# The last 1024 down columns of an MLP go pair by pair in three of four cycles, and two vector operations are merged

## The chip, the cores and the metric

The kernel runs on one core of a Trainium2 chip as one program. Engines: TensorE (PE in the profile, its weight loads PEld), VectorE (DVE), ScalarE (ACT), GpSimd (POOL), and SyncE (SP), whose queue issues nearly all DMA transfers. PE reads its operands from SBUF and writes its sums to PSUM, which has eight banks of 128 x 512 fp32 numbers. The metric is the device time of one execution in microseconds (us); less is better.

## The reference, cut to what matters

A two-layer encoder trunk on x of 256 positions by 2048 channels, all fp32. Each layer has a mixer (not touched here) and then this MLP, with D_FF = 8192:

```python
def sq_relu_mlp(h, w_up, w_down):
    a = jnp.einsum('bsd,df->bsf', h, w_up)
    a = jnp.square(jax.nn.relu(a))
    return jnp.einsum('bsf,fd->bsd', a, w_down)
...
        x = x + sq_relu_mlp(rmsnorm(x, mlp_norm[i]), w_up[i], w_down[i])
    return rmsnorm(x, final_norm)
```

## The kernel before

**Precision.** Products are made in three matmuls each (mm3, L105): every operand is split into a rounded high part and the rest (hi, lo), and hi x hi, hi x lo, lo x hi are summed in one bank. ACT makes the high part (L73, L184), DVE subtracts it (L74, L185). So each weight loaded costs ACT one cast and DVE one subtraction.

**The MLP** (L631) runs twice, once a layer. Hidden columns are made in tiles of 128 ("up tile": accT, L655 to L685, one bank, 16 matmuls of 512 and 16 of 256 columns) and two such tiles make a pair q of 256 hidden rows (hidden, L695: scale, square, split, and the block sums xh, xl of a seven-product scheme). 32 pairs are taken in G = 4 cycles of C = 8. The down product of a pair is a 2 x 2 by 2 x 2 block product: two halves of hidden rows k, two halves of positions t (128 each), two column tiles n of 512. For the first 1024 of the 2048 output columns it is made by seven block products instead of eight (Q1, P2, Q3, Q5, Q7, Q6, Q4; L801 to L818), 21 matmuls, from the weight blocks (bh, bl, made in s_load, L722) and their sums (th, tl, made in s_sums, L733: four DVE additions in place in sraw, then two splits). They stay in seven banks for the whole cycle: four of the pool accp, three of the pool tpp, whose fourth bank is left to the up tiles. A step of the loop L793 is: up tile, three products of the pair before, second up tile, four products. After a cycle s_end (L751) copies Q1 with ACT and adds the seven banks to x with 12 DVE operations.

**The last 1024 columns** come after that (L821): for each of two column tiles n, `linear` (L110) goes over the cycle's 16 k-tiles with two sums of 512 columns (one for each t), 96 matmuls, then add_x (L224) adds the two banks to x. So 192 matmuls a cycle. A weight load is 1 MB (four k-tiles) and is split in two pieces of 1024 columns. In the last cycle one of its eight pairs goes by `rest` (L766), and in the last MLP the last column tile is done in halves with the final norm behind it (Final, L587). The final norm's gain gf is loaded by the POOL queue into a pool of its own before the last MLP (L1152 to L1154).

**What sets the order.** The program is laid out once, when it is built: a planner goes by the order of the text, but puts an instruction ahead on its engine's queue when its inputs and its buffer are there and earlier ones still wait. At run time each engine takes its queue in that fixed order and waits on semaphores. What can go ahead is set by buffers: three raw weight tiles, four hi and four lo pieces (L50 to L52), four staging tiles (tag stg), one each of sraw, bh, bl, th, tl, xh and xl, and eight banks.

Of the kernel before, what the change touches and what calls it, by code (L numbers as in the profile page):

```python
# [19 lines left out]
P = 128  # L20
# [8 lines left out]
PIECE = 2048  # L29
HALF = 1024  # L30


# [4 lines left out]
WHOLE = (1, 2)  # L37

SMALL = ["conv_w", "conv_b", "ln_g", "ln_b", "g_o", "conv_c", "q_g", "kv_g", "g_m0", "g_m1"]
SMALL_N = [8 * CONVK, 8, 8, 8, 16, 8 * 3, 4, 2, 16, 16]  # L40
# [3 lines left out]
def trunk_kernel(ctx, tc, x_in, x_t, small, w_in_e0, w_in_e, w_out_e, w_in_o, w_lat2, w_uqn, w_uqr, w_ukv, w_out_o,  # L44
                 w_up0, w_up1, w_ds0, w_ds1, w_dn0, w_dn1, g_fin, dft_s, dft_c, rope, out):
    nc = tc.nc
# [186 lines left out]
    class NormIn:  # L233


        def __init__(self, name, g):
            self.name, self.g = name, g
            self.act = act_tiles(16, name)
            self.ss = new_ss(name)
            self.r = None  # L240
# [346 lines left out]
    class Final:  # L587


        def __init__(self, gf):  # L590
            self.gf = gf
            self.ss = const.tile([P, 2, 5], F32, name="nfs")
            nc.vector.memset(self.ss[:, 0, 4:], 0.0)

        def part(self, t, i, a, b, gain=True):
# [34 lines left out]

    def mlp(ni, pend, w_up, w_ds, w_dn, nxt):  # L631

# [62 lines left out]
        def hidden(q, z):  # L695
# [13 lines left out]
            nc.vector.tensor_tensor(out=x[:, 3, :], in0=h[:, 3, :], in1=x[:, 2, :], op=ALU.subtract)  # L709
            xh = mp_.tile([P, 4, P], F32R, tag="xh", name="xh")  # L710
            xl = mp_.tile([P, 4, P], F32R, tag="xl", name="xl")
            split_from(x, xh, xl)
# [8 lines left out]

        def s_load(q):  # L722

            raw = mp_.tile([P, PIECE], F32, tag="sraw", name="sraw")
            nc.sync.dma_start(out=raw, in_=w_ds[q])
            bh = mp_.tile([P, 3, 512], F32R, tag="bh", name="bh")
            bl = mp_.tile([P, 3, 512], F32R, tag="bl", name="bl")
            r4 = raw.rearrange("p (a b) -> p a b", a=4)
            for a, b in ((0, 1), (1, 3)):
                split_from(r4[:, a + 1:b + 1, :], bh[:, a:b, :], bl[:, a:b, :])  # L730
            return r4, bh, bl

        def s_sums(r4):  # L733
            for o, i0, i1 in ((1, 1, 0), (0, 0, 2), (2, 1, 2), (3, 2, 3)):
                nc.vector.tensor_tensor(out=r4[:, o, :], in0=r4[:, i0, :], in1=r4[:, i1, :], op=ALU.add)  # L735
            th = mp_.tile([P, 4, 512], F32R, tag="th", name="th")
            tl = mp_.tile([P, 4, 512], F32R, tag="tl", name="tl")
            for a in (0, 2):
                split_from(r4[:, a:a + 2, :], th[:, a:a + 2, :], tl[:, a:a + 2, :])
            return th, tl  # L740
# [7 lines left out]
        def add(out, a, b, op=ALU.add):  # L748
            nc.vector.tensor_tensor(out=out, in0=a, in1=b, op=op)

        def s_end(b):  # L751


            v = stg.tile([P, 512], F32, tag="stg", name="cv", bufs=4)
            nc.scalar.copy(out=v, in_=b["Q1"])
            for q, t, n in (("Q1", 1, 0), ("P2", 1, 0), ("Q3", 1, 1), ("Q5", 1, 1), ("Q5", 0, 1)):
                add(xc(t, n), b[q], xc(t, n))
            u = stg.tile([P, 512], F32, tag="stg", name="cu", bufs=4)
            add(v, b["Q6"], v, ALU.subtract)
            add(u, b["Q7"], v, ALU.subtract)  # L760
            add(xc(0, 0), b["Q4"], xc(0, 0))
            add(xc(1, 1), xc(1, 1), v)
            add(xc(0, 0), xc(0, 0), u)
            add(xc(0, 1), xc(0, 1), u, ALU.subtract)

# [23 lines left out]
        for g in range(G):  # L789
# [29 lines left out]
            s_end(b)  # L819
            hT = [tuple(pair(g * C + k // 2)[:, i, (k % 2) * S:(k % 2 + 1) * S] for i in range(2)) for k in range(2 * C)]  # L820
            for n in (2, 3):  # L821
                if last and n == 3 and isinstance(nxt, Final):
                    linear(hT, list(range(16)), w_dn[2 * g + n - 2], 0, 512, halves=True, done=nxt.last, early=8)
                    st.close()
                    return {}
                acc = linear(hT, list(range(16)), w_dn[2 * g + n - 2], 0, 512, hooks=pend)
                add_x(acc, n)
                if last and n == 2:
                    rest(hT)
                    for m in (0, 1, 2):  # L830
                        nxt.stats(m)
                        pend[4 * m + 3] = [lambda m=m: nxt.chunk(m)]
                elif last:
                    nxt.stats(3)
                    pend = {3: [lambda: nxt.chunk(3)]}
# [31 lines left out]
    nxt = Lazy("n2", smv("g_o"))  # L867
    pend = mlp(ni, pend, w_up0, w_ds0, w_dn0, nxt)
    ni = nxt
# [281 lines left out]

    fp = ctx.enter_context(tc.tile_pool(name="fin", bufs=1))  # L1152
    gf = fp.tile([P, D], F32, name="gf")
    nc.gpsimd.dma_start(out=gf, in_=g_fin.broadcast_to([P, D]))  # L1154

    mlp(ni, pend, w_up1, w_ds1, w_dn1, Final(gf))


# [85 lines left out]
```

## Time and profile before

| | |
|---|---|
| median of 3 runs | 1956.17 us (1955.97 to 1957.41) |
| the profiled execution | 1957.39 us, span 1955.6 us |
| PE busy | 1943.4 us (99%), 9894 matmuls |
| PEld busy | 1651.3 us (84%) |
| DVE busy | 1569.8 us (80%), 2191 instructions |
| ACT busy | 1129.3 us (58%), 1579 instructions |
| POOL busy | 10.8 us (1%) |
| granted clock | 0.999 of full |
| HBM read | 370.27 MB, 190 GB/s over the span |

The span is what the profiler recorded on the core; the execution's own time has 1.8 us around it. Busy times are shares of the span of each engine by itself; engines work side by side. A matmul row shows when it was issued and a modelled length of 0.39 us that overlaps the next, so what one costs is read from the distance between starts. In a timeline, `x4` is a merged run of four, the bracket says how long the engine was idle ahead and what ended that.

### The profile page before, as it was taken

The numbers are of one execution on the slowest core, as the hardware profiler recorded it, in microseconds if no ns is written. First come the engines' busy times: TensorE is split into PE (matmuls) and PEld (weight loads), VectorE is DVE, ScalarE is ACT, GpSimd is POOL, SyncE is SP. The second block draws the span as 40 slices with busy tenths as digits, with TensorE's granted clock in tenths as the row PEclk, the third lists the DMA queues.
The fourth block names the chain that finished last, engine by engine and source line by source line (L and its number), as shares of the span: only waits on it lengthen the run. The fifth ranks groups of instructions, "written<-read, shape, count | busy, mean of one in ns | idle before, by whom it ended". The sixth has DMA issues, their size and how long they took to land.

```text
span 1955.6 us, 25251 instructions
## 1 busy us (share of the span) xinstructions
PE 1943.4 (99%) x9894; PEld 1651.3 (84%) x9894; DVE 1569.8 (80%) x2191; ACT 1129.3 (58%) x1579; POOL 10.8 (1%) x19
## 2 busy tenths in 40 slices
PE   9999999999999999999999999999999999999998
PEld 8887788888888888888888888888888888888887
DVE  7999778978896897887576666588968878896885
ACT  6787656645654664565554545466546645654653
POOL 0000000000000000000000000000000000000000
PEclk9999999999999999999999999999999999999999
DMA  8654555555556555454554546555565555555543
GB/s 294 213 173 162 207 191 194 194 196 183 201 188 211 197 197 199 174 198 167 164 183 146 189 169 242 191 173 196 191 215 194 195 200 187 194 192 207 185 169 129
DMA packets 55207, 374.00 MB, mean 191 GB/s; under 512 B 6064, under 2 KB 6448, under 8 KB 11824
## 3 DMA queue, kind: packets, MB, share of 16 engines
q1 hardware_dynamic: 54656, 370.69, 54.0%
q8 instruction: 77, 1.26, 0.3%
q0 software_dynamic: 144, 1.05, 0.1%
q10 hardware_dynamic: 288, 0.66, 0.1%
q14 instruction: 42, 0.34, 0.1%
HBM read 370.27 MB, written 2.10 MB: 190 GB/s over the span
## 4 chain that ended last, share of the span: by engine, by line
PE 97%; DMA 1%; DVE 1%; issue 0%; ACT 0%; SPq 0%; POOL 0%; POOLq 0%; DVEq 0%; ACTq 0%
PE accT L672 24%; PE acc L107 14%; PE acc L108 14%; PE acc L106 14%; PE accT L664 13%; PE Q L106 4%; PE Q L108 4%; PE Q L107 4%; PE tp L106 1%; PE tp L107 1%; PE tp L108 1%; PE P L107 1%; PE P L106 1%; PE P L108 1%; DMA raw<-in_w_in_e 1%; PE tp L197 1%
## 5 line engine op out<-in xcount | busy, mean ns | idle before, releaser
L74 DVE TENSOR_TENSOR wlo<-raw,whi 128x1024 fp32r<-128x1024 f32 (+1 forms) x572 | 687.9, 1210 | 300.3 <-ACT whi L73 299.8
L73 ACT CAST whi<-raw 128x1024 fp32r<-128x1024 f32 (+1 forms) x572 | 596.5, 1044 | 456.6 <-PE acc L108 291.3
L672 PE MATMUL accT<-n,whi 128*128 128x512 f32 x2048 | 512.5, 392 | 0.0
L672 PEld LDWEIGHTS accT<-n,whi 128*128 128x128 f32 x2048 | 376.1, 188 | 75.1
L664 PEld LDWEIGHTS accT<-n,wlo 128*128 128x128 f32 x2048 | 262.9, 191 | 10.1
L664 PE MATMUL accT<-n,wlo 128*128 128x256 f32 x2048 | 266.4, 283 | 0.0
L107 PE MATMUL acc<-wlo,hT 128*128 128x512 f32 (+1 forms) x544 | 209.6, 385 | 0.1
L108 PE MATMUL acc<-whi,hT 128*128 128x512 f32 (+1 forms) x544 | 208.9, 384 | 0.0
L106 PE MATMUL acc<-whi,hT 128*128 128x512 f32 (+1 forms) x544 | 208.1, 384 | 0.0
L106 PE MATMUL acc<-whi,n 128*128 128x512 f32 (+2 forms) x480 | 180.3, 377 | 2.1 <-ACT whi L73 2.1
L108 PE MATMUL acc<-whi,n 128*128 128x512 f32 (+2 forms) x480 | 177.8, 371 | 0.0
L107 PE MATMUL acc<-wlo,n 128*128 128x512 f32 (+2 forms) x480 | 177.3, 370 | 0.1
L735 DVE TENSOR_TENSOR sraw<-sraw 128x512 f32<-128x512 f32 x248 | 169.4, 683 | 1.0
L185 DVE TENSOR_TENSOR tl<-sraw,th 128x1024 fp32r<-128x1024 f32 x124 | 150.8, 1216 | 0.2
L684 ACT COPY z<-accT 128x256 f32<-128x256 f32 x128 | 48.0, 375 | 156.3 <-PE accT L672 156.3
L184 ACT CAST th<-sraw 128x1024 fp32r<-128x1024 f32 x124 | 128.5, 1044 | 6.1 <-DVE sraw L735 3.2
L185 DVE TENSOR_TENSOR bl<-sraw,bh 128x512 fp32r<-128x512 f32 x124 | 114.7, 952 | 16.5 <-ACT bh L184 16.2
L107 PEld LDWEIGHTS acc<-wlo,hT 128*128 128x128 f32 x544 | 102.2, 188 | 22.4 <-DVE wlo L74 2.3
L106 PEld LDWEIGHTS acc<-whi,hT 128*128 128x128 f32 x544 | 102.2, 188 | 20.9
L108 PEld LDWEIGHTS acc<-whi,hT 128*128 128x128 f32 x544 | 102.2, 188 | 20.4
L184 ACT CAST bh<-sraw 128x512 fp32r<-128x512 f32 x124 | 97.5, 834 | 28.4 <-DMA sraw<-in_w_ds 22.7
L106 PEld LDWEIGHTS acc<-whi,n 128*128 128x128 f32 x480 | 90.4, 189 | 16.3 <-ACT whi L73 2.8
(289 smaller groups left out, 2533.2 us busy)
## 6 DMA issues: line engine op xcount, KB each, us to landing
raw<-in_w_up SPq DMA_DIRECT2D x128, 1024.0 KB, 4.8
raw<-in_w_dn SPq DMA_DIRECT2D x64, 1024.0 KB, 4.9
sraw<-in_w_ds SPq DMA_DIRECT2D x62, 1024.0 KB, 4.8
raw<-in_w_in_o SPq DMA_DIRECT2D x28, 1024.0 KB, 4.9
raw<-in_w_in_e SPq DMA_DIRECT2D x20, 1024.0 KB, 5.0
raw<-in_w_out_e SPq DMA_DIRECT2D x16, 1024.0 KB, 4.9
raw<-in_w_out_o SPq DMA_DIRECT2D x16, 1024.0 KB, 4.8
raw<-in_w_in_e SPq DMA_DIRECT2D x6, 512.0 KB, 7.3
```

What stands on the lines that cost most here:

```text
L73: nc.scalar.copy(out=hi[:, :n], in_=raw[:, o:o + n])
L74: nc.vector.tensor_tensor(out=lo[:, :n], in0=raw[:, o:o + n], in1=hi[:, :n].bitcast(F32), op=ALU.subtract)
L106: nc.tensor.matmul(out=outs, lhsT=hi, rhs=rhi, start=first, stop=False)
L107: nc.tensor.matmul(out=outs, lhsT=hi, rhs=rlo, start=False, stop=False)
L108: nc.tensor.matmul(out=outs, lhsT=lo, rhs=rhi, start=False, stop=last)
L184: nc.scalar.copy(out=hi, in_=src)
L185: nc.vector.tensor_tensor(out=lo, in0=src, in1=hi.bitcast(F32), op=ALU.subtract)
L197: nc.tensor.transpose(out=tp[:, j, t * P:(t + 1) * P], in_=src(t, kt), identity=ident)
L664: nc.tensor.matmul(out=acc[:, S:], lhsT=lo[:, k * P:(k + 1) * P], rhs=act[8 * p + k][0], start=False, stop=False)
L672: nc.tensor.matmul(out=acc, lhsT=hi[:, k * P:(k + 1) * P], rhs=act[kt][2], start=kt == 0, stop=kt == 15)
L684: nc.scalar.copy(out=z[:, j, :], in_=acc[:, S:])
L735: nc.vector.tensor_tensor(out=r4[:, o, :], in0=r4[:, i0, :], in1=r4[:, i1, :], op=ALU.add)
```

## The change

In cycles 0 to 2 of both MLPs the two calls of `linear` are replaced by `both`. It takes the cycle's pairs in the order of the string ORDER: P is a pair by eight block products (24 matmuls into the four banks P2, Q3, Q4 and R, one for each (t, n)), S is a pair by the seven products, whose Q1, Q5, Q7 and Q6 lie in four more banks, in tpp, opened at the first S. After the last, s_end adds the eight banks to x (with the copy of Q1, 14 DVE operations). The weights of those columns are laid out in pairs (w_dt), those of the last cycle stay as they were. xh and xl get two buffers. In s_load the split of one and of two blocks becomes one of three; in s_sums the first two of four additions become one that writes two blocks. gf is loaded into the buffer of sraw, in the last MLP's last cycle, behind `rest` in the text.

```diff
+LAST = 6144
...
+ORDER = "PPPPSPPS"
...
-        def __init__(self, gf):
-            self.gf = gf
+        def __init__(self):
             self.ss = const.tile([P, 2, 5], F32, name="nfs")
...
+        def load(self, gf):
+            self.gf = gf
+            nc.gpsimd.dma_start(out=gf, in_=g_fin.broadcast_to([P, D]))
...
-            xh = mp_.tile([P, 4, P], F32R, tag="xh", name="xh")
-            xl = mp_.tile([P, 4, P], F32R, tag="xl", name="xl")
+            xh = mp_.tile([P, 4, P], F32R, tag="xh", name="xh", bufs=2)
+            xl = mp_.tile([P, 4, P], F32R, tag="xl", name="xl", bufs=2)
...
         def xsum(q, i):
             return tuple(v[:, i, :] for v in xs_of[q])
 
-        def s_load(q):
+        def s_load(q, w=w_ds):
 
             raw = mp_.tile([P, PIECE], F32, tag="sraw", name="sraw")
-            nc.sync.dma_start(out=raw, in_=w_ds[q])
+            nc.sync.dma_start(out=raw, in_=w[q])
             bh = mp_.tile([P, 3, 512], F32R, tag="bh", name="bh")
             bl = mp_.tile([P, 3, 512], F32R, tag="bl", name="bl")
             r4 = raw.rearrange("p (a b) -> p a b", a=4)
-            for a, b in ((0, 1), (1, 3)):
-                split_from(r4[:, a + 1:b + 1, :], bh[:, a:b, :], bl[:, a:b, :])
+            split_from(r4[:, 1:, :], bh, bl)
             return r4, bh, bl
 
         def s_sums(r4):
-            for o, i0, i1 in ((1, 1, 0), (0, 0, 2), (2, 1, 2), (3, 2, 3)):
-                nc.vector.tensor_tensor(out=r4[:, o, :], in0=r4[:, i0, :], in1=r4[:, i1, :], op=ALU.add)
+            b12 = r4[:, 0:1, :].broadcast_to([P, 2, 512])
+            nc.vector.tensor_tensor(out=r4[:, 1::-1, :], in0=r4[:, 1:3, :], in1=b12, op=ALU.add)
+            for o in (2, 3):
+                nc.vector.tensor_tensor(out=r4[:, o, :], in0=r4[:, o - 1, :], in1=r4[:, o, :], op=ALU.add)
             th = mp_.tile([P, 4, 512], F32R, tag="th", name="th")
             tl = mp_.tile([P, 4, 512], F32R, tag="tl", name="tl")
             for a in (0, 2):
...
         def add(out, a, b, op=ALU.add):
             nc.vector.tensor_tensor(out=out, in0=a, in1=b, op=op)
 
-        def s_end(b):
+        def s_end(b, m=0):
 
 
             v = stg.tile([P, 512], F32, tag="stg", name="cv", bufs=4)
             nc.scalar.copy(out=v, in_=b["Q1"])
-            for q, t, n in (("Q1", 1, 0), ("P2", 1, 0), ("Q3", 1, 1), ("Q5", 1, 1), ("Q5", 0, 1)):
-                add(xc(t, n), b[q], xc(t, n))
+            for q, t, n in (("R", 0, 1), ("Q1", 1, 0), ("P2", 1, 0), ("Q3", 1, 1), ("Q5", 1, 1), ("Q5", 0, 1)):
+                if q in b:
+                    add(xc(t, m + n), b[q], xc(t, m + n))
             u = stg.tile([P, 512], F32, tag="stg", name="cu", bufs=4)
             add(v, b["Q6"], v, ALU.subtract)
             add(u, b["Q7"], v, ALU.subtract)
-            add(xc(0, 0), b["Q4"], xc(0, 0))
-            add(xc(1, 1), xc(1, 1), v)
-            add(xc(0, 0), xc(0, 0), u)
-            add(xc(0, 1), xc(0, 1), u, ALU.subtract)
+            add(xc(0, m), b["Q4"], xc(0, m))
+            add(xc(1, m + 1), xc(1, m + 1), v)
+            add(xc(0, m), xc(0, m), u)
+            add(xc(0, m + 1), xc(0, m + 1), u, ALU.subtract)
+
+        def both(g, hT):
+
+            names = {(1, 0): "P2", (1, 1): "Q3", (0, 0): "Q4", (0, 1): "R"}
+            b = {n: accp.tile([P, 512], F32, tag="acc", name=n) for n in names.values()}
+            pairs = deque(range(ORDER.count("P")))
+            seven = deque(range(len(pairs), C))
+            opened = False
+            for i, o in enumerate(ORDER):
+                l = i == C - 1
+                if o == "P":
+                    p = pairs.popleft()
+                    raw = load_raw(w_dt[g * C + p], PIECE)
+                    parts = [split_piece(raw, o, HALF) for o in (0, HALF)]
+                    for (t, n), name in names.items():
+                        for k in range(2):
+                            mm_kt({t: b[name]}, t, hT[2 * p + k], parts[k], 1 - n, 512, i == k == 0,
+                                  k == 1 and (l or (name == "R" and not pairs)))
+                else:
+                    p = seven.popleft()
+                    q = g * C + p
+                    f = not opened
+                    if f:
+                        b.update({n: tpp.tile([P, 512], F32, tag="tp", name=n) for n in ("Q1", "Q5", "Q7", "Q6")})
+                    opened = True
+                    e = not seven
+                    r4, bh, bl = s_load(q, w_dt)
+                    prod(b["Q1"], block(q, 1), bh, bl, 0, f, e)
+                    prod(b["P2"], block(q, 3), bh, bl, 2, False, l)
+                    prod(b["Q3"], xsum(q, 3), bh, bl, 1, False, l)
+                    th, tl = s_sums(r4)
+                    prod(b["Q5"], xsum(q, 0), th, tl, 1, f, e)
+                    prod(b["Q7"], xsum(q, 1), th, tl, 0, f, e)
+                    prod(b["Q6"], xsum(q, 2), th, tl, 2, f, e)
+                    prod(b["Q4"], block(q, 2), th, tl, 3, False, l)
+            s_end(b, 2)
 
         def rest(hT):
 
...
                 prod(b["Q4"], block(q - 1, 2), th, tl, 3, f, l)
             s_end(b)
             hT = [tuple(pair(g * C + k // 2)[:, i, (k % 2) * S:(k % 2 + 1) * S] for i in range(2)) for k in range(2 * C)]
+            if not last:
+                both(g, hT)
+                continue
             for n in (2, 3):
-                if last and n == 3 and isinstance(nxt, Final):
-                    linear(hT, list(range(16)), w_dn[2 * g + n - 2], 0, 512, halves=True, done=nxt.last, early=8)
+                if n == 3 and isinstance(nxt, Final):
+                    linear(hT, list(range(16)), w_dn[n - 2], 0, 512, halves=True, done=nxt.last, early=8)
                     st.close()
                     return {}
-                acc = linear(hT, list(range(16)), w_dn[2 * g + n - 2], 0, 512, hooks=pend)
+                acc = linear(hT, list(range(16)), w_dn[n - 2], 0, 512, hooks=pend)
                 add_x(acc, n)
-                if last and n == 2:
+                if n == 2:
                     rest(hT)
+                    if isinstance(nxt, Final):
+                        nxt.load(mp_.tile([P, PIECE], F32, tag="sraw", name="gf"))
                     for m in (0, 1, 2):
                         nxt.stats(m)
                         pend[4 * m + 3] = [lambda m=m: nxt.chunk(m)]
-                elif last:
+                else:
                     nxt.stats(3)
                     pend = {3: [lambda: nxt.chunk(3)]}
         st.close()
...
-    fp = ctx.enter_context(tc.tile_pool(name="fin", bufs=1))
-    gf = fp.tile([P, D], F32, name="gf")
-    nc.gpsimd.dma_start(out=gf, in_=g_fin.broadcast_to([P, D]))
-
-    mlp(ni, pend, w_up1, w_ds1, w_dn1, Final(gf))
+    mlp(ni, pend, w_up1, w_ds1, w_dt1, w_dn1, Final())
...
-        "w_dn0": _chunks(np.ascontiguousarray(i["w_down"][0][:, HALF:]), 16),
-        "w_dn1": _chunks(np.ascontiguousarray(i["w_down"][1][:, HALF:]), 16),
+        "w_dt0": _blocks(i["w_down"][0][:LAST, HALF:]),
+        "w_dt1": _blocks(i["w_down"][1][:LAST, HALF:]),
+        "w_dn0": _chunks(np.ascontiguousarray(i["w_down"][0][LAST:, HALF:]), 16),
+        "w_dn1": _chunks(np.ascontiguousarray(i["w_down"][1][LAST:, HALF:]), 16),
```

## Rows read from the trace of the kernel before

**Rows 1.** The page: busy time and share of each engine, granted clock in 40 slices.

```profile
PE 1943.4 (99%) x9894; PEld 1651.3 (84%) x9894; DVE 1569.8 (80%) x2191; ACT 1129.3 (58%) x1579; POOL 10.8 (1%) x19
...
PEclk9999999999999999999999999999999999999999
```

**Rows 2.** Timeline of PE, stage end: start us, us, engine, line, operation, out<-in, form.

```profile
434.31 0.39 PE L106 MATMUL acc<-whi,hT 128*128 128x512 f32 x1
...
435.67 0.39 PE L106 MATMUL acc<-whi,hT 128*128 128x512 f32 x1
...
436.35 0.84 PE L672 MATMUL accT<-n,whi 128*128 128x512 f32 x3
```

**Rows 3.** Windows: stage, up stage, stage, whole cycle; columns in the first line.

```profile
core 0: us, PE busy (x) PEld busy (x) DVE busy (x) ACT busy (x) POOL busy (x), PEclk, DMA share, GB/s
392.48:436.35 43.87, 43.84 (x194) 35.95 (x193) 31.84 (x38) 19.97 (x21) 0.00 (x0) 1.00 0.56 205
436.35:564.28 127.93, 127.93 (x682) 110.33 (x680) 111.58 (x155) 76.71 (x101) 0.00 (x0) 1.00 0.55 193
564.28:608.35 44.07, 44.07 (x193) 36.00 (x192) 31.82 (x38) 19.94 (x21) 0.00 (x0) 1.00 0.56 203
565.36:737.36 172.00, 172.00 (x874) 146.33 (x873) 143.42 (x192) 96.44 (x122) 0.00 (x0) 1.00 0.56 196
```

**Rows 4.** Weight loads of the stage's kind, and one of their waits (total, times, longest).

```profile
L107 PEld LDWEIGHTS acc<-wlo,hT 128*128 128x128 f32 x544 | 102.2, 188 | 22.4 <-DVE wlo L74 2.3
...
PEld acc L107 <- DVE wlo L74: 2.7, 7, 0.5
```

**Rows 5.** Timeline of the first stage's entry, all engines, from 384 to 406.

```profile
388.39 1.82 DVE L185 TENSOR_TENSOR bl<-sraw,bh 128x512 fp32r<-128x512 f32 x2
...
394.59 0.68 DVE L749 TENSOR_TENSOR xs<-Q,xs 128x512 f32<-128x512 f32 x1
...
398.23 0.68 DVE L749 TENSOR_TENSOR xs<-xs,cv 128x512 f32<-128x512 f32 x1
...
398.83 1.29 DVE L749 TENSOR_TENSOR xs<-xs,cu 128x512 f32<-128x512 f32 x2
...
400.04 4.62 DVE L74 TENSOR_TENSOR wlo<-raw,whi 128x1024 fp32r<-128x1024 f32 x4
...
401.31 0.19 PEld L107 LDWEIGHTS acc<-wlo,hT 128*128 128x128 f32 x1 [0.46 <-DVE wlo L74]
```

**Rows 6.** Groups of DVE by shape: busy us, mean ns, idle before.

```profile
L185 DVE TENSOR_TENSOR bl<-sraw,bh 128x1024 fp32r<-128x1024 f32 x62 | 75.5, 1218 | 0.1
L685 DVE TENSOR_TENSOR z<-accT,z 128x256 f32<-128x256 f32 x128 | 53.3, 417 | 23.4 <-ACT z L684 23.4
L700 DVE SCALAR_TENSOR_TENSOR z<-z,rb 128x512 f32<-128x512 f32 x64 | 43.7, 684 | 0.3
...
L185 DVE TENSOR_TENSOR bl<-sraw,bh 128x512 fp32r<-128x512 f32 x62 | 42.6, 686 | 16.4 <-ACT bh L184 16.2
...
L707 DVE TENSOR_TENSOR x<-h 128x256 f32<-128x256 f32 x64 | 26.6, 416 | 0.0
```

**Rows 7.** Timeline of the first two steps of the next cycle, from 440 to 480.

```profile
441.92 0.39 PE L106 MATMUL Q<-bh,hT 128*128 128x512 f32 x1
...
456.40 0.33 SPq L725 DMA_DIRECT2D sraw<-in_w_ds  x1
...
457.85 0.39 PE L106 MATMUL Q<-bh,hT 128*128 128x512 f32 x1
...
461.33 1.57 ACT L184 CAST bh<-sraw 128x512 fp32r<-128x512 f32 x2 [1.96 <-DMA sraw<-in_w_ds]
```

**Rows 8.** Last cycle, DVE timeline; then gf's DMA issue with us to landing.

```profile
1886.40 1.22 DVE L185 TENSOR_TENSOR tl<-sraw,th 128x1024 fp32r<-128x1024 f32 x1
...
1923.62 1.45 DVE L600 TENSOR_TENSOR xs<-xs,gf 128x512 f32<-128x512 f32 x2 [0.19 <-ACT junk L598]
...
gf<-in_g_fin POOLq DMA_DIRECT2D x1, 1024.0 KB, 8.6
```

More of the change, by code (lines that the diff above doesn't have):

```diff
@@ L44, in trunk_kernel @@
 def trunk_kernel(ctx, tc, x_in, x_t, small, w_in_e0, w_in_e, w_out_e, w_in_o, w_lat2, w_uqn, w_uqr, w_ukv, w_out_o,
-                 w_up0, w_up1, w_ds0, w_ds1, w_dn0, w_dn1, g_fin, dft_s, dft_c, rope, out):
+                 w_up0, w_up1, w_ds0, w_ds1, w_dt0, w_dt1, w_dn0, w_dn1, g_fin, dft_s, dft_c, rope, out):
     nc = tc.nc
@@ L629, in last, with mlp @@
             nc.sync.dma_start(out=ov[:, t, 1152:], in_=xs[:, t, 1152:])
-    def mlp(ni, pend, w_up, w_ds, w_dn, nxt):
+    def mlp(ni, pend, w_up, w_ds, w_dt, w_dn, nxt):
         G, C = 4, 8
@@ L867, in trunk_kernel @@
     nxt = Lazy("n2", smv("g_o"))
-    pend = mlp(ni, pend, w_up0, w_ds0, w_dn0, nxt)
+    pend = mlp(ni, pend, w_up0, w_ds0, w_dt0, w_dn0, nxt)
     ni = nxt
```

## The prediction

> **What bounds the kernel now.** I read the page's busy shares first. TensorE (PE) is busy 99% of the span at full granted clock in every slice, VectorE (DVE) 80% [rows 1]. PE busy time is modelled, so I then took the PE timeline at the end of a stage, where matmuls of one shape follow each other: from 434.31 to 435.67 six 512-column matmuls are issued, so one costs 1.36 / 6 = 0.2267 us [rows 2]. The stage that is changed (L821 to L827, 192 such matmuls) begins at 392.48 and ends where the next up tile begins, 436.35: 43.87 us; the second of the six, cut in the same way at 564.28 and 608.35, is 44.07 us [rows 2, 3]. 192 x 0.2267 = 43.53, so only 0.34 and 0.54 us of them are not matmul slots. The list of waits agrees: in the whole run PE's weight loads wait 2.7 us for a low part from DVE, at most 0.5 us at a time [rows 4]. So PE's own count of slots sets the time, and any slot removed is time removed, as long as DVE still delivers. The windows say how much room DVE has: 31.84 of 43.87 us in this stage, 111.58 of the 127.93 us of the up stage behind it, 143.42 of a whole cycle of 172.00 us [rows 3].
>
> **The change part by part.**
>
> *Matmuls.* A pair by eight products is 4 x 2 x 3 = 24 matmuls, by seven 21. Six and two give 144 + 42 = 186 for 192. Per stage 6 x 0.2267 = 1.36 us, in six stages 8.16 us. Weight loads come one per matmul as before, 188 ns [rows 4] under a slot of 226.7. The moving data stay 512 columns wide, and each pair still takes one 1 MB load, so loads and bytes are the same 8 per stage.
>
> *DVE, amount.* Back to back DVE gives out a 1024-wide subtraction every 4.62 / 4 = 1.16 us and a 512-wide one every 0.60 us (398.23, 398.83) [rows 5]. Gone per cycle: four low parts (4.6 us) and four add_x (2.4). New: two sets of seven-block operands and 14 additions of s_end (8.4). One set has a 1536-wide subtraction, a double sum, two single sums and two 1024-wide subtractions. The 1536-wide one isn't in the trace: 686 to 1218 ns for 512 to 1024 gives 1.04 ns a column, so 1.75 us alone, 1.70 in a queue; below it can't be under the 1.22 of two thirds of it, above not over the 1.90 of the two operations it replaces. The double sum reads a broadcast block and writes two blocks backwards; the row with a backward read (256 wide, 416 ns) and the row with a broadcast (512 wide, 684 ns) cost what plain ones do (417, 686), so 1.16; bounds 0.6 and 2.4 [rows 6]. A set is 1.70 + 1.16 + 1.20 + 2.32 = 6.4 us. The same two merges save about 0.1 us in each of the other eight down pieces. Sum per cycle: -4.6 - 2.4 + 12.8 + 8.4 - 1 = +13.2 us. 143.4 + 13.2 = 156.6 of 170.6 us: 92%, still below PE. ACT casts three blocks in 1.57 us [rows 7], so about 0.5 a block: two sets of seven blocks, one copy, less four pieces of two blocks, 14 + 1 - 8 = 7 blocks or 3.7 us more on 96.4 of 172 [rows 3].
>
> *DVE, place.* Count from the start of the stage (t = 0, which is 392.48): pairs end at 5.4, 10.9, 16.3 and 21.8, the first seven-block step at 26.5, two pairs at 37.4, the last seven-block step at 42.2. Until t = 7.6 DVE is busy with the s_end of the first 1024 columns and the hidden tile, as now; PE runs 36 matmuls on the three low parts ready at the start, goes on with what is ready in the other bank, and waits 0.46 us for the fourth [rows 5]. In the new order the fourth part is wanted earlier (in the second half of the second pair's first group), but there are four banks to go on in, 16 matmuls or 3.6 us from t = 5.4, that is to 9.1; the part arrives at 8.8. The four banks come from the old s_end in the order Q3, Q5, Q1, P2; Q1's is read until 395.27 (t = 2.8) and the third group wants it at t = 2.7 [rows 5]. I take the same 0.34 us for the entry of the first stage; bounds 0 and 1.5 (if the queue order doesn't use the other banks). From 7.6 DVE has nine low parts (10.4), the rest of the first set (4.7; its first part is done ahead, as today's next down piece has its bl at 388.39 [rows 5]), xl of the last hidden tile (0.6; it now waits until the first seven-block step has read the old one, which costs only one of four staging buffers), the second set (6.4), one addition (0.6), two low parts of the next up tile (2.3): 25.0, done by t = 32.6 against 37.4. The stage itself fits.
>
> *The exit.* Here is the new risk. Before, two additions stood between the last product and the next cycle; now 13 additions follow the closing of Q1 at t = 38.1. They take 7.8 us and end near 45.5. Only then come, in order of the program, the low parts of the next down piece, its sums, the remaining low parts of the up tile. PE's next up tile takes 441.92 - 436.35 = 5.57 us [rows 2, 7], so its first down product wants bl at 47.7; DVE has it at 47.2. Low parts of the second up tile: wanted 51.6 and 52.5, there 51.1 and 52.2. The sums' low parts: wanted 55.35, there 54.5. The single sraw buffer then goes to the next load: 4.9 us to the next cast as now (456.40 to 461.33), one cast over all three blocks 1.57 at most, subtraction 1.7, ready 62.7; a step lasts 457.85 - 441.92 = 15.93 us [rows 7], so it is wanted at 63.7. Four margins of 0.3 to 1.0 us. Each semaphore hop or misplaced instruction comes off them. I take 0.3 us of PE waiting at the exit; bounds 0 and the 4.6 us by which DVE's work of that step exceeds 15.93 (13.9 of its own, 15.93 x 111.58 / 127.93 [rows 3], and eleven additions of s_end, 6.6).
>
> *gf.* The POOL queue now loads it into sraw after the last set of the last cycle has been read (1886.40 + 1.22), beside work that doesn't need it. It lands in 8.6 us and is first read at 1923.62 [rows 8]. Nothing; without the cover, 8.6 us once. POOL has nothing else queued until the end.
>
> *Sum.* Stage 42.17 + 0.34 + 0.3 = 42.8 for 43.87; 1.05 x 6 = 6.3 us off. The profiled execution took 1957.39 us with a span of 1955.6; the same 1.8 around it gives 1951.1 for an execution like it. The median is 1.2 lower, 1956.17, so 1949.9, rounded 1950.
>
> **The rivals.** (a) *Exit waits eat it.* Stalls of 1.36 us a stage cancel the gain; the four margins are smaller than that, so DVE 1.5 to 2 us later (one more addition ahead of bl plus a late cast) is enough. For: the up stage behind would have DVE at about (111.6 + 6.4 + 6.6 - 2.2) / 127.9 = 96%. Against: work has been placed ahead freely so far. Exit waits of 1.0 to 1.7 us: 1956.17 - 8.2 + 6.0 to 10.2 = 1954 to 1958.
>
> (b) *DVE becomes the bound at the exit: slower.* If s_end stands as a block in front of the next cycle's first step, the excess of 4.6 us becomes PE idle time in each of six places: 1956.17 - 8.2 + 27.6 = 1975.6; at half of it 1962. It decides from an excess of 1.36 us at PE. For: DVE executes in order, and sraw, bh, bl, th, tl have one buffer each, so a late set makes the next load late too. Against: about 5 us of DVE idle time before t = 37.4 can take low parts ahead, and the step is preceded by an up tile whose operands are there.
>
> (c) *No wait at all.* Margins hold and the entry wait goes too: 8.2 to 10.2 off, 1946 to 1948.
>
> (d) *The clock falls.* The eight banks are in turn now in the up stage too (four sums, three, and the up tile), with a clock of 1.00 [rows 3]. If brief stops at the exit took it to the lower level for one seven-block step a stage, 21 slots of 0.2267 would double: +4.8 x 6 - 8.2 = 1976.5. The Trainium skill has this in "TensorE: Matmul & The Clock Gate", section "A second HAM failure mode: psum-queue depth-cycling": a kernel that cycled through PSUM banks paused often enough between groups for the clock to go up and down. This trace disagrees so far (clock 1.00 in windows that do so).
>
> That the change doesn't remove what it says I exclude by the count of 186.
>
> **How the numbers follow.** My forecast (6.3 off, own range 1947.5 to 1952.2): 0.55. (c) 0.07. (a) 0.26. (b) 0.11, (d) 0.01. A difference of 0.2% (3.9 us) is about what a measurement of this kernel can tell from none. Faster than 1952.3: 0.55 + 0.07 = 0.62; within: (a) 0.26; slower than 1960.1: 0.12. The range for 8 in 10 takes the forecast, the upper part of (c) and all of (a): 1947 to 1958.5.
>
> **What the profile would show.** Right: 186 matmuls between the last th product and the next accT, 42.2 to 43 us long; waits of weight loads for wlo, bl or tl under 0.7 us per stage; DVE near 92% of a cycle; gf landed before it is read. Wrong: PE's weight loads waiting for bl, tl or wlo just behind each changed stage by over 1.4 us (then (a) or (b)); an xs addition that a first product of the next cycle waits for; a window below clock 1.00; a 1536-wide subtraction over 1.9 us or a double sum near 2.4.

## The result, and the profile after

The changed kernel takes 1983.22 us (median of 4 runs, 1981.75 to 1984.42) where the kernel before takes 1956.16: a ratio of 1.0134 [1.0122, 1.0146], 27 us slower. The forecast was 6 us faster. The profiled execution took 1981.75 us with a span of 1980.0.

The busy shares, and the chain that ended last by engine:

```profile
PE 1952.0 (99%) x9858; PEld 1640.2 (83%) x9858; DVE 1650.2 (83%) x2163; ACT 1147.2 (58%) x1535; POOL 10.7 (1%) x19
...
PEclk9999999999999999999999999999999999999999
...
PE 85%; DVE 8%; DMA 4%; ACT 2%; issue 1%; SPq 0%; POOL 0%; POOLq 0%; DVEq 0%; ACTq 0%
```

PE has 36 instructions fewer than in [rows 1], as the change says (six stages, six matmuls each), and the granted clock is full in every slice. PE still looks 99% busy, which shows how little that share tells: its ends are modelled, and short waits hide in it. The chain does show them: it is 85% PE now, with DVE, DMA and ACT at 14% together, where the same line of the kernel before reads:

```profile
PE 97%; DMA 1%; DVE 1%; issue 0%; ACT 0%; SPq 0%; POOL 0%; POOLq 0%; DVEq 0%; ACTq 0%
```

The windows that answer to [rows 3], first changed stage, the up stage behind it, second changed stage (us, then busy time of PE, PEld, DVE, ACT, POOL, granted clock, DMA share, GB/s):

```profile
392.37:434.77 42.40, 42.40 (x187) 34.94 (x186) 36.52 (x43) 20.51 (x23) 0.00 (x0) 1.00 0.54 196
434.77:570.95 136.18, 131.16 (x681) 109.35 (x680) 121.01 (x150) 78.62 (x94) 0.00 (x0) 1.00 0.50 180
570.95:613.69 42.74, 42.74 (x188) 34.94 (x186) 37.32 (x43) 22.61 (x24) 0.00 (x0) 1.00 0.59 218
...
434.77:613.69 178.92, 173.90 (x868) 144.28 (x866) 158.33 (x192) 101.23 (x117) 0.00 (x0) 1.00 0.52 189
```

The stage that was changed did what was forecast: 42.40 and 42.74 us for a forecast 42.8, against 43.87 and 44.07. The loss is in the up stage behind it, here 136.18 us for 127.93, whose matmuls the change doesn't touch. A cycle (from the first up product to that of the next cycle) is 178.92 us for 172.00; if only the slots went it would be 172.00 - 1.36 = 170.64.

PE's weight loads say what they wait for (total us, times, longest):

```profile
PEld Q L111 <- DVE bl L189: 19.6, 34, 1.3
PEld accT L680 <- DVE z L693: 9.9, 8, 1.3
PEld Q L111 <- DVE tl L189: 4.7, 5, 1.2
PEld Q L110 <- ACT bh L188: 3.6, 7, 0.8
PEld acc L111 <- DVE wlo L78: 1.2, 3, 0.5
```

Lines have moved by 4 to 8: L78, L111, L189, L680 and L693 are L74, L107, L185, L672 and L685 of before. The row that I had watched, for wlo, fell from 2.7 to 1.2 us; six of its seven waits before stood in the stages that were changed, and none of the three left does. What is new is a wait for bl, 34 times in the 62 down pieces of the up stages: in six of them 1.25 us or a little more, in the other 28 between 0.4 and 0.5. So it is not one wait at a stage's exit but one in most of the pieces that follow. DVE has room there, 121.01 of 136.18 us; it delivers late without being full.

One piece with the long wait, all engines, from 502 to 520 (start, us, engine, line, operation; in brackets the idle time before and what ended it):

```profile
504.02 0.33 SPq L733 DMA_DIRECT2D sraw<-in_w_ds  x1
...
508.89 1.48 ACT L188 CAST bh<-sraw 128x1536 fp32r<-128x1536 f32 x1 [0.32 <-DMA sraw<-in_w_ds]
...
510.41 1.76 DVE L189 TENSOR_TENSOR bl<-sraw,bh 128x1536 fp32r<-128x1536 f32 x1 [0.50 <-ACT bh L188]
...
512.08 0.42 DVE L693 TENSOR_TENSOR z<-accT,z 128x256 f32<-128x256 f32 x1
512.22 0.19 PEld L111 LDWEIGHTS Q<-bl,hT 128*128 128x128 f32 x1 [1.25 <-DVE bl L189]
...
512.42 1.22 DVE L742 TENSOR_TENSOR sraw<-sraw 128x1024 f32<-128x1024 f32 x1
...
513.67 1.06 ACT L188 CAST th<-sraw 128x1024 fp32r<-128x1024 f32 x1 [1.61 <-DVE sraw L742]
...
516.42 0.68 DVE L744 TENSOR_TENSOR sraw<-sraw 128x512 f32<-128x512 f32 x1
...
517.14 1.06 ACT L188 CAST th<-sraw 128x1024 fp32r<-128x1024 f32 x1 [0.35 <-DVE sraw L744]
518.23 1.23 DVE L189 TENSOR_TENSOR tl<-sraw,th 128x1024 fp32r<-128x1024 f32 x1
519.48 0.33 SPq L733 DMA_DIRECT2D sraw<-in_w_ds  x1
```

Read it as a ring. The load into the one sraw buffer lands, ACT casts all three blocks, DVE subtracts all three, the double sum overwrites the blocks that were just subtracted, th is cast from the sums, tl is subtracted, and only then may the next load start, 0.02 us after the last tl. From the cast's start it takes 512.17 - 508.89 = 3.28 us until there is any bl, and 3.53 until the first sum starts. In the kernel before, the two casts of [rows 7] from 461.33 are one of a single block and one of two; behind the first come

```profile
461.99 0.69 DVE L185 TENSOR_TENSOR bl<-sraw,bh 128x512 fp32r<-128x512 f32 x1 [1.35 <-ACT bh L184]
462.71 0.69 DVE L735 TENSOR_TENSOR sraw<-sraw 128x512 f32<-128x512 f32 x1
```

The first bl is there 1.35 us after the cast's start, and the first sum starts 1.38 after it. The merged operations are no slower than the ones they replace (1.76 us for 0.69 + 1.22, 1.22 for two of 0.69); the *first* result of each comes some 2 us later, in a chain that closes on itself.

The loads into sraw show the pace of this ring. In the kernel before they are issued at 456.40, 473.31, 490.05, 506.06, 522.08, 538.09 and 554.10: the last four steps are 16.0 us each, the rate at which PE takes pieces. In the changed kernel (SP's timeline):

```profile
431.02 0.33 SPq L733 DMA_DIRECT2D sraw<-in_w_ds  x1
449.44 0.33 SPq L733 DMA_DIRECT2D sraw<-in_w_ds  x1
469.29 0.33 SPq L733 DMA_DIRECT2D sraw<-in_w_ds  x1
486.66 0.33 SPq L733 DMA_DIRECT2D sraw<-in_w_ds  x1
...
552.04 0.33 SPq L733 DMA_DIRECT2D sraw<-in_w_ds  x1
```

That is 18.42, 19.85 and 17.37 us, and (552.04 - 431.02) / 7 = 17.29 on the mean. This cycle starts slowest: before the ring has settled, PE's weight loads also wait three times 1.34 us for z and twice over 1.1 us for tl. The last two steps take 16.27 and 16.29 us, and in the next cycle six in a row take 16.25 to 16.30. One such settled turn:

```profile
661.13 0.33 SPq L733 DMA_DIRECT2D sraw<-in_w_ds  x1
...
670.16 0.19 PEld L111 LDWEIGHTS Q<-bl,hT 128*128 128x128 f32 x1 [0.46 <-DVE bl L189]
...
676.17 1.23 DVE L189 TENSOR_TENSOR tl<-sraw,th 128x1024 fp32r<-128x1024 f32 x1
677.42 0.33 SPq L733 DMA_DIRECT2D sraw<-in_w_ds  x1
```

A turn of the ring, with the casts and low parts of the up tiles that stand between its operations in the queues of ACT and DVE, is 16.29 us long where PE needs 16.0. So the ring sets the pace, and PE's weight load waits for bl in each turn. That it is the one buffer which closes it is tested below (e8).

### The profile page after: what moved, and what is told of

The parts are those of the page before. It is cut to its first block, busy times and chain, and to the rows that moved or that the text cites. A ratio compares the mean times of both kernels' runs of the same rounds, so it can differ in the third digit from the quotient of the medians.

```text
span 1980.0 us, 25092 instructions
## 1 busy us (share of the span) xinstructions
PE 1952.0 (99%) x9858; PEld 1640.2 (83%) x9858; DVE 1650.2 (83%) x2163; ACT 1147.2 (58%) x1535; POOL 10.7 (1%) x19
## 3 DMA queue, kind: packets, MB, share of 16 engines
q8 instruction: 77, 1.26, 0.2%
## 4 chain that ended last, share of the span: by engine, by line
PE 85%; DVE 8%; DMA 4%; ACT 2%; issue 1%; SPq 0%; POOL 0%; POOLq 0%; DVEq 0%; ACTq 0%
PE accT L680 19%; PE accT L672 10%; PE acc L111 9%; PE acc L112 9%; PE acc L110 9%; PE Q L111 6%; PE Q L112 6%; PE Q L110 5%; DMA sraw<-in_w_ds 3%; DVE wlo L78 2%; PE P L111 2%; PE P L112 2%; DVE bl L189 2%; PE P L110 1%; DVE tl L189 1%
## 5 line engine op out<-in xcount | busy, mean ns | idle before, releaser
L78 DVE TENSOR_TENSOR wlo<-raw,whi 128x1024 fp32r<-128x1024 f32 (+2 forms) x548 | 657.6, 1209 | 174.1 <-ACT whi L77 172.1
L77 ACT CAST whi<-raw 128x1024 fp32r<-128x1024 f32 (+2 forms) x548 | 567.9, 1043 | 347.5 <-PE acc L112 159.2
L680 PE MATMUL accT<-n,whi 128*128 128x512 f32 x2048 | 517.2, 393 | 6.5 <-DVE z L693 6.5
L680 PEld LDWEIGHTS accT<-n,whi 128*128 128x128 f32 x2048 | 375.8, 188 | 85.0 <-DVE z L693 9.9
L672 PEld LDWEIGHTS accT<-n,wlo 128*128 128x128 f32 x2048 | 264.3, 191 | 11.4
L672 PE MATMUL accT<-n,wlo 128*128 128x256 f32 x2048 | 268.0, 283 | 0.0
L189 DVE TENSOR_TENSOR tl<-sraw,th 128x1024 fp32r<-128x1024 f32 x148 | 180.1, 1218 | 0.2
L111 PE MATMUL acc<-wlo,n 128*128 128x512 f32 (+2 forms) x480 | 177.4, 371 | 0.1
L189 DVE TENSOR_TENSOR bl<-sraw,bh 128x1536 fp32r<-128x1536 f32 x74 | 129.9, 1756 | 38.4 <-ACT bh L188 36.0
L188 ACT CAST bh<-sraw 128x1536 fp32r<-128x1536 f32 x74 | 109.4, 1479 | 41.4 <-DMA sraw<-in_w_ds 27.9
L110 PEld LDWEIGHTS acc<-whi,n 128*128 128x128 f32 x480 | 90.2, 189 | 16.1 <-ACT whi L77 2.6
L112 PEld LDWEIGHTS acc<-whi,n 128*128 128x128 f32 x480 | 90.3, 188 | 15.5
L111 PEld LDWEIGHTS acc<-wlo,n 128*128 128x128 f32 x480 | 90.5, 189 | 13.9 <-DVE wlo L78 0.3
L742 DVE TENSOR_TENSOR sraw<-sraw 128x1024 f32<-128x1024 f32 x74 | 90.0, 1216 | 0.1
L111 PE MATMUL Q<-tl,xh 128*128 128x512 f32 x222 | 87.1, 392 | 2.8 <-DVE tl L189 2.8
L110 PE MATMUL Q<-th,xh 128*128 128x512 f32 x222 | 86.7, 393 | 0.4 <-ACT th L188 0.4
L112 PE MATMUL Q<-th,xl 128*128 128x512 f32 x222 | 86.9, 391 | 0.0
```

Of the source, the lines that this page charges most:

```text
L77: nc.scalar.copy(out=hi[:, :n], in_=raw[:, o:o + n])
L78: nc.vector.tensor_tensor(out=lo[:, :n], in0=raw[:, o:o + n], in1=hi[:, :n].bitcast(F32), op=ALU.subtract)
L110: nc.tensor.matmul(out=outs, lhsT=hi, rhs=rhi, start=first, stop=False)
L111: nc.tensor.matmul(out=outs, lhsT=hi, rhs=rlo, start=False, stop=False)
L112: nc.tensor.matmul(out=outs, lhsT=lo, rhs=rhi, start=False, stop=last)
L188: nc.scalar.copy(out=hi, in_=src)
```

## The experiments

Ratios are against the kernel before, run on the same chip; its medians there are 1957.2 to 1957.6 us (single runs 1955.8 to 1959.7).

**Which part costs the time.** In e1 the change stays and both merges are undone; e2 is the kernel before with the two merges alone.

```diff
-            split_from(r4[:, 1:, :], bh, bl)
+            for a, b in ((0, 1), (1, 3)):
+                split_from(r4[:, a + 1:b + 1, :], bh[:, a:b, :], bl[:, a:b, :])
...
-            b12 = r4[:, 0:1, :].broadcast_to([P, 2, 512])
-            nc.vector.tensor_tensor(out=r4[:, 1::-1, :], in0=r4[:, 1:3, :], in1=b12, op=ALU.add)
-            for o in (2, 3):
-                nc.vector.tensor_tensor(out=r4[:, o, :], in0=r4[:, o - 1, :], in1=r4[:, o, :], op=ALU.add)
+            for o, i0, i1 in ((1, 1, 0), (0, 0, 2), (2, 1, 2), (3, 2, 3)):
+                nc.vector.tensor_tensor(out=r4[:, o, :], in0=r4[:, i0, :], in1=r4[:, i1, :], op=ALU.add)
```

> The changed kernel with s_load and s_sums as they were before (two casts and subtractions, four sums); both() and the rest stay. Theory M (the merged operations lengthen the chain DMA of sraw, cast, subtraction, sums, next DMA, so that PE waits for bl in nearly every step): most of the 27 us go away, 1950 to 1958, bl waits of PE's weight loads under 5 us. Theory X (the 14 additions at the exit of the changed stage put DVE behind, and it doesn't recover): stays near 1978 to 1983, since only some 0.1 us of DVE work per step changes. Theory MX (late exit starts it, the longer chain keeps it): 1955 to 1968, waits in the first two or three steps of a cycle only.

> The kernel before with the two merges alone. M: 62 steps each wait about 0.4 us for bl, 1956 + 15 to 25 = 1971 to 1981. X: 1956 within 2. MX: 1956 to 1962, as the first up stage of the changed kernel, which has no changed stage ahead of it, took 130 us as before.

Measured: e1 1960.16 us, 1.0017 [1.0007, 1.0026]; e2 1969.24, 1.0063 [1.0048, 1.0078]. The merges are 23 of the 27 us: 1983.22 - 1960.16. Alone in the kernel before they cost 12. And e1 shows a second loss: without the merges the change should have had its 8 us and is 3 us slower. Its waits for bl are down to 6.1 us; its cycle is 172.29 us, 1.65 more than 170.64, and the larger waits of that cycle (0.3 to 0.6 us) lie in the first two steps behind the changed stage. So the exit takes back 1.65 us where 0.3 was forecast: rival (a). Of the theories, e1 fits MX, 2 us above M's range; e2 lies between those of MX and M, and not for M's reason: its weight loads don't wait for bl, but 10.0 us for z (8 times) and 6.2 us for xl (16 times).

How the merge stops PE in e2, which has no changed stage (timeline):

```profile
532.26 1.48 ACT L184 CAST bh<-sraw 128x1536 fp32r<-128x1536 f32 x1 [3.59 <-DMA sraw<-in_w_ds]
533.77 1.76 DVE L185 TENSOR_TENSOR bl<-sraw,bh 128x1536 fp32r<-128x1536 f32 x1 [2.69 <-ACT bh L184]
...
535.45 0.42 DVE L685 TENSOR_TENSOR z<-accT,z 128x256 f32<-128x256 f32 x1
...
535.92 3.68 PE L672 MATMUL accT<-n,whi 128*128 128x512 f32 x8 [1.83 <-DVE z L685]
```

ACT had been idle 3.59 us for the load; DVE stood idle 2.69 us in front of bl. Behind bl in DVE's fixed queue is z, which empties the up tile's bank, and PE waits 1.83 us for that bank. So a late load reaches PE through an operation that has nothing to do with the load. The eight matmuls behind the wait take longer, too; the last section shows the granted clock there.

**Which merge.** e6 undoes the load's merge only, e7 that of the sums only.

> The changed kernel with the split of s_load in two again (block 1, then blocks 2 and 3), the merged double sum kept. Theory A (the cast and subtraction over three blocks are the price: bl of the first product comes 1.9 us later after the DMA, since 1.48 + 1.76 stand where 0.62 + 0.69 stood, and z behind bl in DVE's queue holds PE's only free bank): near 1960 to 1966. Theory B (the double sum is the price: it can't begin until the whole bl has been read, and th's first cast waits for it): near 1975 to 1983.

> The changed kernel with four single sums again, the merged split of s_load kept. A: 1975 to 1983. B: 1960 to 1966. If each merge has a part, e6 and e7 both lie between 1964 and 1977.

Measured: e6 1963.03, 1.0032 [1.0019, 1.0045]; e7 1971.24, 1.0075 [1.006, 1.009]. Over e1 the sums' merge alone costs 2.9 us, the load's merge alone 11.1, both 23.1: more than their sum. A ring that has some slack until it has none would do that; no run shows it by itself. e6 is in A's range and e7 between A's and B's, so the load's merge is the larger part and the sums' merge has one of its own. In e7 PE still waits 22.3 us for bl; in e6 that is down to 1.7, and 16.6 us of waits for z are left, 40 times at most 0.8.

**Is it the ring?** If the merges cost only because sraw has one place, a second place should make them free. There is no room for a second sraw buffer, but the ring of up pieces has buffers of the same size, so every other down piece is loaded into one of these: e8 is the changed kernel with that, e9 the same without merges, e13 the kernel before with merges and two places, e15 the kernel before with two places alone.

```diff
-            raw = mp_.tile([P, PIECE], F32, tag="sraw", name="sraw")
-            nc.sync.dma_start(out=raw, in_=w[q])
+            if q % 2:
+                raw = load_raw(w[q], PIECE)
+            else:
+                raw = mp_.tile([P, PIECE], F32, tag="sraw", name="sraw")
+                nc.sync.dma_start(out=raw, in_=w[q])
```

> The changed kernel, merges kept, but every second down piece is loaded into a raw weight tile (three of them) instead of the one sraw buffer, so the next load needn't wait for the last reading of the one before. If the price is the closed chain through the one sraw buffer (DMA, cast, subtraction, sums, cast, subtraction, next DMA), the bl waits go: 1950 to 1962. If it is DVE's amount of work or the order in its queue, or if the up tiles now lack raw tiles, it stays at 1975 or more.

> No merges, and two places for the down pieces. If the 1.6 us that each up stage behind a changed stage gives back in e1 come from the late sraw load too, 1948 to 1953, faster than before. If they come from DVE's 14 additions as work, as e1: 1958 to 1962. Over 1965: raw tiles are short.

> The kernel before with the two merges (e2, 1969) and the two places for the down pieces. Ring theory: the 12 us of e2 go away without both() too, 1954 to 1958. If the merges cost by themselves (a longer way to the first bl, z behind bl in the queue), 1963 to 1970.

> The kernel before with two places for the down pieces and nothing else. It had no bl or tl waits to lose, so 1955 to 1957.5; if it gains 2 us or more, then part of what e8 and e9 show is not recovered loss of the change but a gain of its own.

Measured: e8 1954.06, 0.9985 [0.9976, 0.9995]; e9 1954.48, 0.9984 [0.9974, 0.9993]; e13 1955.01, 0.9991 [0.9982, 1.0]; e15 1955.69, 0.9991 [0.9981, 1.0]. The ring theory holds: with two places the merges cost nothing, in the changed kernel (e8 beside e9) and in that of before (e13 beside e15), where they had cost 23 and 12 us. e8 has no wait for bl at all. Two places by themselves are worth about 1.6 us, with an interval that ends at none (1.0).

But e9 is only 1.2 us below e15, with 36 slots less (8.2 us). So the exit's loss stands by itself, and e9 falls between its two ranges.

**Does the exit lose by the order?** e3 and e5 put the two seven-block steps earlier, e3 with the merges and e5 without:

```diff
-ORDER = "PPPPSPPS"
+ORDER = "PPSPPSPP"
```

> The changed kernel with ORDER PPSPPSPP: the same products, the seven-product pairs third and sixth, so that Q1, Q5, Q7 and Q6 close 11 us before the end and only P2, Q3, Q4 and R are open at the exit. M: 1975 to 1985, the bl waits stay. X: the waits go, 1948 to 1955. MX: between, 1952 to 1968.

> Both of these: no merges, ORDER PPSPPSPP. M: as e1. X: as e3. MX: the shortest of the four, 1947 to 1953 (6 x 1.36 us under before, with 0 to 5 us of waits).

Measured: e3 1982.02, 1.0132 [1.0117, 1.0147]; e5 1972.79, 1.0082 [1.0065, 1.0099]. A miss: with one place, earlier sevens do nothing in e3 and cost 12.6 us over e1 in e5. Its weight loads wait up to 1.3 us for z and for tl, 4 times each, and 8.0 us in small waits for bl; I have not followed these to their start.

e14 keeps e9's order of pairs and banks but gives all eight pairs eight products, so the 192 matmuls are back and s_end is four plain additions:

```diff
-ORDER = "PPPPSPPS"
+ORDER = "PPPPPPPP"
...
-            s_end(b, 2)
+            for (t, n), name in names.items():
+                add(xc(t, 2 + n), b[name], xc(t, 2 + n))
```

> e9 with ORDER PPPPPPPP and four plain additions at the end: pair by pair, but no seven-product pairs, so 192 matmuls and 4 instead of 14 additions at the exit. X': the up stages behind take 123.3 us as before, the changed stages 43.9 to 44.1, 1954 to 1957 in all. If pair by pair costs by itself (entry waits for four banks, both pieces wanted at once), 1958 or more.

Measured: 1955.59, 0.999 [0.9981, 0.9999], a cycle of 171.81 us, e15's 171.82. So going pair by pair through the banks costs nothing; what costs is what the seven-block steps bring.

e9's exit, DVE's timeline and one weight load of PE (its first up product is at 433.49; only some rows of it stand here, but DVE has no gap from 428.83 to 450.66):

```profile
433.50 1.28 DVE L760 TENSOR_TENSOR xs<-Q,xs 128x512 f32<-128x512 f32 x2
...
437.09 1.28 DVE L760 TENSOR_TENSOR xs<-xs,cu 128x512 f32<-128x512 f32 x2
438.29 1.82 DVE L189 TENSOR_TENSOR bl<-sraw,bh 128x512 fp32r<-128x512 f32 x2
...
446.78 1.22 DVE L189 TENSOR_TENSOR bl<-raw,bh 128x1024 fp32r<-128x1024 f32 x1
447.91 1.22 DVE L189 TENSOR_TENSOR tl<-sraw,th 128x1024 fp32r<-128x1024 f32 x1
...
449.18 0.19 PEld L111 LDWEIGHTS Q<-tl,xh 128*128 128x128 f32 x1 [0.90 <-DVE tl L189]
```

The additions of s_end run until 438.3, then the low parts and sums of the next down piece, with the next but one's bl between the two halves of tl. PE waits 0.90 us for the second half, in the whole run 5.2 us in 6 times. Another 1.9 us in 6 times go to xl, 0.32 at 473.66 in this cycle. Together that is the loss: e9's cycle is 171.68 us, 1.22 more than e15's 171.82 less the six slots.

**Two ways to shorten it.** e12 gives e9's last three additions, which need no bank, to GpSimd:

```diff
+            eng = nc.gpsimd if m else nc.vector
+            for t, n, w, op in ((1, 1, v, ALU.add), (0, 0, u, ALU.add), (0, 1, u, ALU.subtract)):
+                eng.tensor_tensor(out=xc(t, m + n), in0=xc(t, m + n), in1=w, op=op)
```

> e9 (no merges, two places) with the last three additions of the changed stage's s_end, which read SBUF only, on GpSimd. Theory X' (what is left of the loss, about 1 us in each up stage behind a changed stage, is DVE's 14 additions ahead of the next bl, sums and tl): 1.8 us less on DVE there is more than the 0.9 us of tl wait, so 1947 to 1952. If the wait is set by the order (ring, buffers) and not by DVE's work, 1953 to 1956. If GpSimd slows DVE's reads beside it, over 1956.

Measured: 1958.41, 1.0006 [0.9996, 1.0015], 4 us worse than e9; the last section has its rows.

e16 is e9 with another order: it closes the seven-block steps' own banks (Q1, Q5, Q7, Q6) one pair earlier. e18 has, besides, s_end take these four first and the banks that close last (P2, Q3, Q4, R) at the end; e19 is e18 with the merges and e20 is e18 with the sevens one pair earlier still (PPSPPSPP). All have two places.

```diff
-ORDER = "PPPPSPPS"
+ORDER = "PPPSPPSP"
```

> e9 (no merges, two places; 1954.5) with ORDER PPPSPPSP: the four seven-product banks close 5.4 us before the exit, s_end in its old order. If the tl wait of 0.9 us behind each changed stage is due to additions that can't start before the last products, 1949 to 1952; if the chains on x (R first, then Q5; Q3 first, then Q5 and v) hold the other additions back all the same, 1953 to 1957.

> As e16, and s_end of the changed stage in another order: first all that the seven products' banks give, then P2, Q3, Q4 and R, so that four additions (2.4 us) are left at the exit in place of 13. Exit theory: the tl wait goes, 1947 to 1951. If it stays at 1953 to 1957, the loss behind the changed stages isn't the additions at the exit but DVE's amount of work (the seventh step now stands where the low parts for the exit were made).

> e18 with the merged operations: with two places the merges cost nothing (e8 against e9), so as e18 within 2 us.

> e18 with ORDER PPSPPSPP: the second set is asked for another 5.4 us earlier, the first as well, when DVE still has the first s_end to do. Exit theory: as e18, or 1 to 3 us more for an entry wait. Amount theory: 1953 to 1957.

Measured: e16 **1948.89**, 0.9955 [0.994, 0.997]; e18 1949.27, 0.9956 [0.9941, 0.9971]; e19 1950.57, 0.9964 [0.995, 0.9978]; e20 1949.35, 0.9958 [0.9943, 0.9972]. The four are one result within their intervals, and each beats both kernels. The cycles of e16 and e18, a window each:

```profile
433.77:604.62 170.85, 170.85 (x867) 145.07 (x866) 157.85 (x212) 98.86 (x128) 0.00 (x0) 1.00 0.55 197
```

```profile
434.16:604.85 170.69, 170.69 (x868) 145.25 (x866) 158.12 (x212) 99.81 (x127) 0.00 (x0) 1.00 0.55 197
```

170.69 us for the 170.64 that the kernel before leaves without loss; e15's cycle, with its two places, would leave 170.46. In e18 the additions for the seven-block banks start at 427.05, ahead of the stage's end, and the first whole bl is there at 436.1 for 440.0 in e9. So against e15 a cycle gains 1.13 us (e18) and 0.97 us (e16) of the 1.36 that the slots were priced at, and one pair of products behind the last seven-block step covers most of what its additions cost. No wait of PE's weight loads for bl or tl is left in either.

## Why the prediction was wrong

**Matmuls: right.** 186 in the stage, 42.40 and 42.74 us for 42.8, no wait for a weight's low part in them. Once the waits are gone, e18 shows 1.31 us less a cycle than the kernel before (172.00 - 170.69), 1.13 less than e15, for the 1.36 forecast.

**DVE, amount: nearly right, and it misled.** A cycle holds 158.33 us of DVE work in the changed kernel and 158.12 in e18, for a forecast 156.6. That forecast has a wrong count in it: s_end makes 12 additions in the changed stage and 11 in the kernel before, not 14 and 12, so by its own prices the sum is 1.2 us less, 155.4, and the miss 3 us of 158. The two operations that weren't in the trace came out as estimated (1.75 and 1.16 forecast), in DVE's groups by shape (busy us, mean ns):

```profile
L189 DVE TENSOR_TENSOR bl<-sraw,bh 128x1536 fp32r<-128x1536 f32 x74 | 129.9, 1756 | 38.4 <-ACT bh L188 36.0
...
L742 DVE TENSOR_TENSOR sraw<-sraw 128x1024 f32<-128x1024 f32 x74 | 90.0, 1216 | 0.1
```

The same row holds the fault: 36.0 us of DVE waiting for ACT's bh ahead of it, where [rows 6] has 16.2 for the split one.

**The step that failed** is the sentence "The same two merges save about 0.1 us in each of the other eight down pieces". It prices a merge as an amount of DVE time, where DVE had time to spare, and not as a delay in the chain load, cast, bl, sums, tl, load. Both ends of each price in that paragraph are lengths of operations; none is the 2 us by which the first result comes later. In place of 0.1 us saved in each of these pieces, PE's weight loads wait 0.4 to 0.5 us for bl in 28 pieces and 1.25 in six, and the chain turns in 16.25 to 16.30 us at best for the 16.0 that PE needs. The merges cost 23.1 us (e1), and nothing as soon as the chain is opened (e8, e13). The exit's fourth margin did count the merged cast and subtraction, but for one step only: it had the second piece of the cycle ready at 62.7 for 63.7, so its load at 62.7 - 1.7 - 1.57 - 4.9 = 54.5. Measured it was issued at 449.44 - 392.37 = 57.1, and up to 552.04 the steps took 17.29 us on the mean.

The Trainium skill bears on this in "Perfetto Trace Analysis", section "Optimizing Scalar/DVE Operations": grouping into larger operations can help where the engine is saturated, and where it isn't but causes gaps on other engines, breaking instructions up may let work finish sooner. The runs agree: DVE was at 83%, and splitting the two operations again gave back 23.1 us.

**The exit: a term mis-sized.** Forecast 0.3 us a stage, measured 1.65 in e1 and 171.68 - 170.64 = 1.04 in e9 (1.22 beside e15). The forecast had the sums' low parts at 54.5, that is 12.0 us behind the stage's end at 42.5; in e9 the last of them is there at 449.13 - 433.49 = 15.6. It is later although the forecast had two additions too many in front of it (11 follow the close of Q1, not 13). The rest of the work was all listed, but my queue ended with what PE wanted first; the planner's has up-tile low parts and the following piece's bl in between. So rival (a) was the true account of the change without its merges, with DVE later than its condition asked for (3.6 us for 1.5 to 2) and a part of that covered; its 1954 to 1958 holds e9 and ends 2 us below e1.

**Rival (b)** gave a slower time for a reason that wasn't the one: s_end does stand at the exit, but its excess costs 1 to 1.65 us, not 4.6. **(c)** is near what e16 and e18 are, with another order and two places, at 1949 in place of its 1946 to 1948. **(d)**: in the changed kernel the granted clock is 1.00 in every window, changed stage and exit included, so it has no part in the 27 us. But the clock can fall behind stops of PE: e2 and e19 show it once each (last section).

**gf: right.** It is issued on POOL's queue at 1919.9 and first read at 1947.48, when it had long landed:

```profile
1947.48 1.45 DVE L607 TENSOR_TENSOR xs<-xs,gf 128x512 f32<-128x512 f32 x2 [0.19 <-ACT junk L605]
```

**Open.** The cycle behind the first changed stage loses more than the one behind the second (178.92 and 174.09 us). In the second, PE's weight loads wait 0.75 us for bh, 1.26 once for bl and then 0.41 to 0.46 a piece; the three waits of 1.34 us for z and the two for tl are in the first alone. Why the two cycles start so differently was not traced. Why e5 is worse than e1 is open too.

## What to carry to other kernels

Before merging two operations, ask who waits for the first half of the result: on an engine with time to spare a merge saved nothing here (e8 beside e9), and in a chain that closes through a single buffer (the next load waits for the last reader) its delay can be paid in every turn. Count the length of that ring beside the time in which the bound engine uses up a piece; where they are close, open the ring first (a second place) and merge after. And work that follows the last product of a stage needs products behind it as cover: here one pair moved behind the last seven-block step turned a gain of 1.4 us (e9 over e15) into one of 7 (e16 over e15, both by their ratios to the kernel before).

## What the runs showed of the hardware

**GpSimd's additions slowed DVE's beside them.** In e12 three 512-wide additions run on GpSimd (its timeline, where POOL's lengths are rough):

```profile
436.51 1.32 POOL L776 TENSOR_TENSOR xs<-xs,cv 128x512 f32<-128x512 f32 x1 [180.94 <-DVE cv L760]
437.78 3.98 POOL L776 TENSOR_TENSOR xs<-xs,cu 128x512 f32<-128x512 f32 x2
```

DVE's own operations in and behind that time:

```profile
437.55 3.06 DVE L189 TENSOR_TENSOR bl<-sraw,bh 128x512 fp32r<-128x512 f32 x2
...
440.53 1.79 DVE L746 TENSOR_TENSOR sraw<-sraw 128x512 f32<-128x512 f32 x1
...
443.71 0.68 DVE L746 TENSOR_TENSOR sraw<-sraw 128x512 f32<-128x512 f32 x1
```

The pair of bl takes 3.06 us where e9 has 1.82, the sum behind it 1.79 where it is 0.68 once GpSimd is done. So three additions of 0.6 us taken off DVE cost it 1.24 + 1.11 = 2.35 us elsewhere, and PE's waits for tl rise from 5.2 to 9.6 us. The Trainium skill has a rule that fits in "GPSIMD Engine Reference", section "1. Specifications": GpSimd's SBUF interfaces are shared with VectorE, with contention for DVE instructions that have two SBUF inputs. These do, and the rows agree.

**Behind stops of PE its granted clock fell, in two runs.** In e2 the stop before 535.92 (PE's last matmul was issued at 533.69) is followed by eight matmuls that take 3.68 us. The next group of the same eight takes 2.00:

```profile
541.36 2.00 PE L672 MATMUL accT<-n,whi 128*128 128x512 f32 x8
```

The window from 536 to 539 has the granted clock at 0.50, the lower of its two levels; from 533 to 534 and from 540 to 541 it is 1.00:

```profile
536.00:539.00 3.00, 3.00 (x7) 2.35 (x8) 3.00 (x4) 1.58 (x2) 0.00 (x0) 0.50 0.16 57
```

So this stop cost its 1.83 us and some 1.7 more. In e19, near the start of the kernel, two stops of 0.63 and 0.84 us stand before matmuls issued at 13.65 and 15.00, and the granted clock is 0.50 from 15.3 to 18.0; e18 stops for 0.23 and 0.85 us in the same place and stays at 1.00. The stops of PE in the changed kernel's up stages, 0.9 us at most, did not bring the clock down.
